# First layer's down projection by seven block products, its weight sums by DMA, conditioning sums re-spread

## The chip, the core and the metric

The kernel runs on one core of one Trainium2 chip. It works with five engines: TensorE (PE in the profile, its weight loads PEld), VectorE (DVE), ScalarE (ACT), GpSimd (POOL) and SyncE (SP), which here only issues transfers. The metric is the time of one execution on the device in microseconds (us). It is read two ways: as the median of unprofiled runs, and from one profiled execution, whose span runs from the first to the last instruction.

## What is computed

Two layers of a diffusion backbone on 512 tokens of width 1024, all float32. Layer 0 mixes the tokens by a long convolution and by neighbourhood attention, layer 1 by a conformer convolution; behind each follows a ConvFFN. Cut to what matters here:

```python
def conv_ffn(t, w_up, w_dw, b_dw, w_down):
    z = dwconv(t @ w_up, w_dw, b_dw)
    g, u = jnp.split(z, 2, axis=-1)
    return (jax.nn.silu(g) * u) @ w_down

for layer in range(DEPTH):
    shift1, scale1, gate1, shift2, scale2, gate2 = adaln_params(c, w_mod[layer], b_mod[layer])
    hn = rms_norm(h, g_mix_pre[layer]) * (1 + scale1) + shift1
    ...
    h = h + gate1 * rms_norm(y, g_mix_post[layer])
    hn = rms_norm(h, g_ffn_pre[layer]) * (1 + scale2) + shift2
    y = conv_ffn(hn, ffn_w_up[layer], ffn_w_dw[layer], ffn_b_dw[layer], ffn_w_down[layer])
    h = h + gate2 * rms_norm(y, g_ffn_post[layer])
```

The inner width D_FF is 2816 = 22 x 128, so the down projection multiplies 512 x 2816 by 2816 x 1024.

## The kernel before

**Products in three matmuls.** A float32 operand is split into a high and a low part of a faster format, and a product is taken as high x high + high x low + low x high (`mm3`, L285 to L289). So each block product of 128 x 128 by 128 x 512 is three matmuls on TensorE, on lines L287, L288 and L289.

**Weights.** They come as a stream `ws` of units of 128 x 1024 floats (512 KB): `load` (L298) has SP bring a unit from memory into one of three `raw` tiles, and `split` (L306, L310) has ACT write the high part and DVE the low part, into a pool `w` of eight tiles. `ws.get(n)` hands out the next unit and splits n more ahead. Loads of the conditioning use the same three `raw` tiles.

**Conditioning.** Shifts, scales and gates are products of one vector with a matrix. They are not done on TensorE but as sums on DVE (`gemv_acc`, L489), one 512 KB load and one instruction for each piece, so that they lie beside other work. `mod_cols` makes shift and scale (loads named wcol), `mod_gate` a gate (loads named wgate, a bias row `binit`, a gain `gp`). They are generators in a list `bg`; `bg_step()` advances the first one by a step, and calls of it are strewn over the program.

**Stages.** After the prologue: the mixer's up projection (to about 135 us, with the norm of 256 context tokens in between), the filter transforms, the attention (about 222 to 291), its output projection (to 345), the first layer's ffn (up projection to 583.4, down projection to 704.9), the conformer (to 857), the second layer's ffn (up projection 865 to 1122, down projection to 1228). In the attention each of 16 units of work has scores on TensorE, an exponential on ACT, a normalisation of the tile P on POOL (L1293) in two halves, transposes of P on TensorE (L1299) and the product with V; TensorE's order is written out by hand there.

**The down projection, two ways.** In the first layer it is `gemm_td`: 22 weight units, for each 4 chunks of tokens x 2 halves of the width x 3 matmuls, with the last six units kept so that the chunks finish one after the other. In the second layer it is `down_fast`, a scheme of seven products instead of eight (Strassen's, in Winograd's form): tokens, inner width and output width are halved, and seven products of half-size blocks, combined by additions, replace eight. Each product runs through 11 pieces of the inner width x 2 token chunks x 3 matmuls, `parts` splits the activations for them (tiles named gs), and DVE and ACT add the results (m, s6, sx, sw) to y. It needs sums of activation blocks, which `blocks` makes on DVE during the up projection (tiles ee and dd, and gu in place), and four sums of weight blocks.

**Weight sums.** `sums_down` makes these in memory by transfers alone: SP copies a block (L358) into a buffer, and POOL issues a transfer that adds a second block onto it (L363), 24 copies and 24 accumulating transfers in six column groups. It is a generator in `bg`, too, and runs during the second layer's up projection. POOL's transfer waits until its copy has landed. POOL and SP take their instructions in order, so what stands behind a waiting instruction waits as well.

**Who orders.** Apart from stretches ordered by hand (the attention and `down_fast` on TensorE), a scheduler places instructions on each engine mainly in the order of the program.

## Time and profile before

| | us |
|---|---|
| median of 3 runs | 1240.96 (1240.25 to 1241.71) |
| the profiled execution | 1239.77 |
| its span | 1238.0 |
| first layer: up projection | about 345 to 583.4 |
| first layer: down projection | 583.4 to 704.9 |
| second layer: up projection | about 865 to 1122 |
| second layer: down projection | 1122 to 1228 |

The granted TensorE clock is 0.997 over the span. 203.55 MB move by DMA, 164 GB/s in the mean, most of it weights. Rows of the timeline have start, length, engine, line, operation, output <- input with shapes, a count where neighbours were put together, and in brackets the idle time before and what ended it. An engine's name with a q (SPq) is its instruction queue, where transfers are issued. A transfer's row on SP or POOL is the time to issue it; it lands later.

### The profile page before, as it was taken

How to read it: one execution, taken by the hardware profiler on the slowest of the kernel's cores; microseconds unless marked ns; L12 is line 12 of the kernel's file. 1: busy time of each engine (PE TensorE's matmuls, PEld its weight loads, DVE VectorE, ACT ScalarE, POOL GpSimd, SP SyncE). 2: the span in 40 equal slices, each digit the busy share in tenths (PEclk: the TensorE clock that was granted, in tenths of full speed). 3: DMA queues.
4: the chain of work that ended last, by engine and by line, in shares of the span. 5: the costliest groups of instructions: out<-in, count | busy, mean ns of one | idle time of the engine just before them, and what ended most of it. 6: DMA issues, size and time to landing. Idle time of an engine off the chain costs nothing.

```text
span 1238.0 us, 15798 instructions
## 1 busy us (share of the span) xinstructions
PE 1222.3 (99%) x6024; PEld 1016.8 (82%) x6024; DVE 872.7 (70%) x1203; ACT 539.0 (44%) x856; POOL 104.7 (8%) x175
## 2 busy tenths in 40 slices
PE   9999999999999999999999999999999999999996
PEld 6688888888898888888888888888988888888885
DVE  6577795876657788878624656787688665667677
ACT  6543334575443333345324443233453333346554
POOL 3300000231200000000000100001100111110002
PEclk9999999999999999999999999999999999999998
DMA  9546334843126477765335152022258889864663
GB/s 349 206 131 190 122 102 139 255 160 120 52 86 221 157 252 253 240 203 170 102 110 180 50 182 68 4 66 86 69 202 240 244 249 250 234 180 136 188 204 128
DMA packets 57883, 203.55 MB, mean 164 GB/s; under 512 B 6859, under 2 KB 6987, under 8 KB 57808
## 3 DMA queue, kind: packets, MB, share of 16 engines
q1 hardware_dynamic: 53988, 190.29, 46.4%
q0 software_dynamic: 3632, 11.93, 5.5%
q8 instruction: 47, 0.77, 0.3%
q10 hardware_dynamic: 188, 0.33, 0.1%
q14 instruction: 28, 0.23, 0.1%
HBM read 199.64 MB, written 25.17 MB: 182 GB/s over the span
## 4 chain that ended last, share of the span: by engine, by line
PE 86%; DVE 7%; DMA 4%; issue 2%; ACT 1%; POOL 0%; SPq 0%; DVEq 0%; POOLq 0%; ACTq 0%
PE pz L287 15%; PE pz L288 15%; PE pz L289 15%; PE acc L289 5%; PE acc L287 5%; PE acc L288 5%; PE pg L287 2%; PE pg L288 2%; PE pg L289 2%; DMA raw<-in_wcol 2%; PE m L287 2%; PE m L288 2%; PE m L289 2%; PE po L1319 1%; DVE w L310 1%
## 5 line engine op out<-in xcount | busy, mean ns | idle before, releaser
L288 PE MATMUL pz<-hTl,w 128*128 128x512 f32 (+1 forms) x920 | 345.4, 376 | 0.0
L287 PE MATMUL pz<-hTh,w 128*128 128x512 f32 (+1 forms) x920 | 344.7, 377 | 0.5 <-DVE hTh L580 0.5
L289 PE MATMUL pz<-hTh,w 128*128 128x512 f32 (+1 forms) x920 | 345.1, 376 | 0.0
L310 DVE TENSOR_TENSOR w<-raw,w 128x1024 fp32r<-128x1024 f32 x179 | 215.0, 1205 | 172.9 <-ACT w L306 170.7
L306 ACT CAST w<-raw 128x1024 fp32r<-128x1024 f32 x179 | 185.0, 1037 | 322.8 <-PE pz L288 139.6
L289 PEld LDWEIGHTS pz<-hTh,w 128*128 128x128 f32 x920 | 173.8, 189 | 31.4
L288 PEld LDWEIGHTS pz<-hTl,w 128*128 128x128 f32 x920 | 173.8, 189 | 30.1 <-DVE hTl L581 0.4
L287 PEld LDWEIGHTS pz<-hTh,w 128*128 128x128 f32 x920 | 173.0, 189 | 31.0 <-DVE hTh L580 1.0
L489 DVE SCALAR_TENSOR_TENSOR acc<-raw,sc,acc 128x1024 f32<-128x1024 f32 x74 | 95.0, 1284 | 39.6 <-DMA raw<-in_wcol 24.5
L1024 ACT ACTIVATE cv<-pz,pk 128x512 f32<-128x512 f32 x88 | 67.6, 772 | 7.7 <-PE pz L289 7.7
L1026 DVE SCALAR_TENSOR_TENSOR cv<-pz,pk,cv 128x511 f32<-128x511 f32 x88 | 65.6, 747 | 1.7
L1025 DVE SCALAR_TENSOR_TENSOR cv<-pz,pk,cv 128x511 f32<-128x511 f32 x88 | 65.2, 745 | 0.3 <-ACT cv L1024 0.2
L1424 ACT ACTIVATE cv<-cv 128x512 f32<-128x512 f32 x44 | 27.7, 629 | 80.1 <-DVE cv L1026 80.0
L287 PE MATMUL m<-w,gs 128*128 128x512 f32 x132 | 51.3, 389 | 0.0
L288 PE MATMUL m<-w,gs 128*128 128x512 f32 x132 | 51.3, 389 | 0.0
L289 PE MATMUL m<-w,gs 128*128 128x512 f32 x132 | 51.3, 389 | 0.0
L310 DVE TENSOR_TENSOR wk<-raw,wk 128x1024 fp32r<-128x1024 f32 (+1 forms) x30 | 35.9, 1205 | 21.8 <-ACT wk L306 21.5
L288 PE MATMUL acc<-w,gs 128*128 128x512 f32 x128 | 49.8, 389 | 0.0
L289 PE MATMUL acc<-w,gs 128*128 128x512 f32 x128 | 49.1, 389 | 0.0
L287 PE MATMUL acc<-w,gs 128*128 128x512 f32 x128 | 48.5, 389 | 0.0
L306 ACT CAST wk<-raw 128x1024 fp32r<-128x1024 f32 (+1 forms) x30 | 30.9, 1037 | 37.4 <-DMA raw<-in_wdn 13.7
L458 POOL TENSOR_SCALAR t<-t,t 128x1 f32<-128x1 f32 x19 | 10.3, 541 | 398.0 <-ACT py L467 389.4
(364 smaller groups left out, 2103.2 us busy)
## 6 DMA issues: line engine op xcount, KB each, us to landing
raw<-in_wup SPq DMA_DIRECT2D x88, 512.0 KB, 4.2
raw<-in_wcol SPq DMA_DIRECT2D x48, 512.0 KB, 4.2
raw<-in_wgate SPq DMA_DIRECT2D x32, 512.0 KB, 4.2
raw<-in_pw SPq DMA_DIRECT2D x24, 512.0 KB, 4.1
raw<-in_wdn SPq DMA_DIRECT2D x22, 512.0 KB, 3.6
raw<-in_win SPq DMA_DIRECT2D x20, 512.0 KB, 3.6
b<-in_wdb SPq DMA_DIRECT2D x20, 512.0 KB, 8.0
raw<-b SPq DMA_DIRECT2D x20, 512.0 KB, 3.6
```

Source lines behind the costliest of these rows:

```text
L287: PE.matmul(o, ah, bh, start=start, stop=False)
L288: PE.matmul(o, ah, bl, start=False, stop=False)
L289: PE.matmul(o, al, bh, start=False, stop=stop)
L306: A.copy(hi, r)
L310: V.tensor_tensor(lo, r, f(hi), op=ALU.subtract)
L458: G.tensor_scalar(v, sums[0], sums[1], EPS, op0=ALU.add, op1=ALU.add)
L489: V.scalar_tensor_tensor(acc, rs[k], ck_, init if k == 0 else acc, op0=ALU.mult, op1=ALU.add)
L1024: A.activation(dst, pz, AF.Identity, bias=pc(bk, i), scale=pc(wk + "1", i))
L1025: V.scalar_tensor_tensor(dst[:, 1:w], pz[:, 0:w - 1], pc(wk + "0", i), dst[:, 1:w], op0=ALU.mult, op1=ALU.add)
L1026: V.scalar_tensor_tensor(dst[:, 0:w - 1], pz[:, 1:w], pc(wk + "2", i), dst[:, 0:w - 1], op0=ALU.mult, op1=ALU.add)
L1319: PE.matmul(po[HALF[e], qs], vt[:, d0:d0 + 64], PT[u // 2][:, e, c, qs], start=first, stop=last)
L1424: A.activation(cv[:, 0], cv[:, 0], AF.Silu, bias=0.0, scale=1.0)
```

## The change

The first layer's down projection also goes by `down_fast`. For this its weights are laid out in blocks as the second layer's are, `sums_down` takes the layer as an argument, and a generator `sums0` of the first layer's sums is advanced by its own calls, from the mixer's up projection to the first layer's up projection. The products of the first layer run in another order ("6213475" against "6217345"; the digits name the seven products). `blocks` now runs in both layers. The two gates and the shift and scale that are computed during the first layer's ffn change places (both gates first), fewer steps are taken per weight unit from the sixteenth step on, a gate's sum accumulates in the tile of its bias, and the gain gp is loaded later. The end of the first layer's ffn allocates the next stage's transposed tiles later (`room`).

```diff
-    wdn = g["ffn_w_down"].reshape(2, NFF, P, D)
-    a["wdn"] = wdn[:1]
-    a["wdb"] = wdn[1].reshape(11, 2, P, 2, 512).transpose(1, 3, 2, 0, 4).reshape(2, 2, P, 11 * 512)
+    wdn = g["ffn_w_down"].reshape(2, 11, 2, P, 2, 512)
+    a["wdb"] = wdn.transpose(0, 2, 4, 3, 1, 5).reshape(2, 2, 2, P, 11 * 512)
...
-    def sums_down():
+    def sums_down(l):
-        b = a["wdb"]
+        b, to = a["wdb"][l], wsum[l]
...
-    PRODUCTS = ("b11_21", "b11_12_21_22", "b11_21_22", (0, 0), (1, 1), "b21_22", (0, 1))
+    PRODUCTS = {"6": "b11_21", "2": "b11_12_21_22", "1": "b11_21_22", "7": (0, 0), "3": (1, 1), "4": "b21_22", "5": (0, 1)}
+    ORDER = ("6213475", "6217345")
...
-        acc = s4(F32, (P, 1024), "acc")
+        acc = s4(F32, (P, 1024), "acc") if init is None else init
...
-        gp = s4(F32, (P, 1024), "gp")
-        SP.dma_start(gp, a["gpost"][l, which - 1].partition_broadcast(P))
         acc = None
         for acc in gemv_acc(a["wgate"][l, which - 1], 8, sc, init=binit):
             yield
+        gp = s4(F32, (P, 1024), "gp")
+        SP.dma_start(gp, a["gpost"][l, which - 1].partition_broadcast(P))
...
+    sums0 = sums_down(0)
+
+    def sums0_step():
+        next(sums0, None)
...
             got.append(u_ev(n, pz))
             bg_step(1)
+            sums0_step()
...
         bg_step(2 if u in (5, 9) else 1)
+        sums0_step()
...
+    bg += [mod_gate(0, 2), mod_gate(1, 1), mod_cols(1, (1, 2))]
...
-            if fast and i % 2:
+            if i % 2:
                 blocks(i // 2)
...
-                bg_step(nbg)
-            if fast and i == NFF - 3:
+                bg_step(nbg - (gi and i >= one))
+                sums0_step()
+            if i == NFF - 3:
                 act_fast(0, 0, keep=True)
+        for _ in sums0:
+            pass
...
-        def act(k):
-            t_ = s4(F32R, n="gs")
-            src = gu[k // 2][:, k % 2]
-            A.copy(t_[:, 0], src)
-            V.tensor_tensor(t_[:, 1], src, f(t_[:, 0]), op=ALU.subtract)
-            return t_[:, 0], t_[:, 1]
-
         bg_drain()
-        gemm_td(NFF, KEEP, act, after, nxt)
+        with tc.manual_schedule(engines={mybir.EngineType.PE}):
+            down_fast(after)
-    bg += [mod_gate(0, 2), mod_cols(1, (1, 2)), mod_gate(1, 1)]
-    after, late2, st2 = stage_end(0, 2, 1, 1)
-    ffn(0, hT, late, after, 4, 2)
+    after, late2, st2 = stage_end(0, 2, 1, 1, room=2)
+    ffn(0, hT, late, after, 4, 2, one=16)
```

What this moves on the engines is shown at four places. First the beginning of the first layer's down projection on PE (lines L286 to L288 after the change are L287 to L289 before); w tiles are weights, gs tiles activations, acc and m are sums in PSUM. Before:

```order
L287 MATMUL acc_5173<-w_5079,gs_5164 128x512
L288 MATMUL acc_5173<-w_5080,gs_5164 128x512
L287 MATMUL acc_5177<-w_5079,gs_5164 128x512
L288 MATMUL acc_5177<-w_5080,gs_5164 128x512
L287 MATMUL acc_5181<-w_5079,gs_5164 128x512
```

and after:

```order
L286 MATMUL m_5284<-w_5179,gs_5091 128x512
L287 MATMUL m_5284<-w_5180,gs_5091 128x512
L288 MATMUL m_5284<-w_5179,gs_5091 128x512
L286 MATMUL m_5284<-w_5179,gs_5091 128x512
L287 MATMUL m_5284<-w_5180,gs_5091 128x512
```

One weight unit served eight sums (acc) before; it serves two (m) now, in a product that has only half of the tokens and of the width. Over the stage the rows with a gs tile go from 528 to 462 (990 to 924 with the second layer's).

Next POOL in the attention. P are the tiles of exponentials that it normalises, qL rows it clears, b_21_0_78 and b_22_0_79 two of the first layer's weight sums. Before:

```order
L1241 MEMSET qL_2229 64x512 x2
L1293 TENSOR_SCALAR P_2106<-P_2106,t_2159 128x512 x2
L1293 TENSOR_SCALAR P_2154<-P_2154,t_2196 128x512 x2
L1293 TENSOR_SCALAR P_2191<-P_2191,t_2289 128x512 x2
L1293 TENSOR_SCALAR P_2284<-P_2284,t_2323 128x512 x2
L1293 TENSOR_SCALAR P_2318<-P_2318,t_2377 128x512 x2
L1241 MEMSET qL_2444 64x512 x2
```

and after:

```order
L1248 MEMSET qL_2247 64x512 x2
L1300 TENSOR_SCALAR P_2123<-P_2123,t_2176 128x512 x2
L363 DMA b_21_0_78<-in_wdb 128x1024
L1300 TENSOR_SCALAR P_2171<-P_2171,t_2214 128x512 x2
L363 DMA b_22_0_79<-in_wdb 128x1024
L1300 TENSOR_SCALAR P_2209<-P_2209,t_2307 128x512 x2
L1300 TENSOR_SCALAR P_2302<-P_2302,t_2342 128x512 x2
L1300 TENSOR_SCALAR P_2337<-P_2337,t_2396 128x512 x2
L363 DMA b_21_0_78<-in_wdb 128x1024
L1248 MEMSET qL_2465 64x512 x2
```

Accumulating transfers now stand between the normalisations of the fourth, fifth and sixth unit and behind that of the eighth.

The copies for which these wait are on SP; raw tiles are loads of wout and wcol, BM the attention's bias. Before:

```order
L298 DMA raw_2141<-in_wcol 128x1024
L1257 DMA BM_2360<-in_rpb 128x1024
L298 DMA raw_2178<-in_wcol 128x1024
L298 DMA raw_2271<-in_wout 128x1024
L298 DMA raw_2486<-in_wout 128x1024
L298 DMA raw_2853<-in_wout 128x1024
```

and after:

```order
L297 DMA raw_2158<-in_wcol 128x1024
L297 DMA raw_2195<-in_wcol 128x1024
L1264 DMA BM_2379<-in_rpb 128x1024
L297 DMA raw_2289<-in_wout 128x1024
L358 DMA b_21_0_78<-in_wdb 128x1024
L358 DMA b_22_0_79<-in_wdb 128x1024
L297 DMA raw_2507<-in_wout 128x1024
L358 DMA b_21_22_0_80<-in_wdb 128x1024
L358 DMA b_12_21_22_0_81<-in_wdb 128x1024
```

The copies come behind the first wout load (raw_2271 before, raw_2289 after) and behind the next one.

Last POOL in the mixer's up projection, at the two context norms (t tiles of one column: a sum and its power of -1/2). Before:

```order
L515 MEMSET binit_768 128x1024
L460 TENSOR_SCALAR t_779<-t_777 128x1
L462 TENSOR_TENSOR t_781<-t_779,nhalf 128x1
L460 TENSOR_SCALAR t_787<-t_785 128x1
L462 TENSOR_TENSOR t_789<-t_787,nhalf 128x1
```

and after:

```order
L514 MEMSET binit_772 128x1024
L363 DMA b_21_0_78<-in_wdb 128x1024
L459 TENSOR_SCALAR t_782<-t_780 128x1
L363 DMA b_22_0_79<-in_wdb 128x1024
L461 TENSOR_TENSOR t_784<-t_782,nhalf 128x1
L459 TENSOR_SCALAR t_790<-t_788 128x1
L461 TENSOR_TENSOR t_792<-t_790,nhalf 128x1
```

One accumulating transfer now stands ahead of the first norm and one in the middle of it.

More of the change, by code (lines that the diff above doesn't have):

```diff
@@ L488, in gemv_acc @@
             else:
-                V.scalar_tensor_tensor(acc, rs[k], ck_, init if k == 0 else acc, op0=ALU.mult, op1=ALU.add)
+                V.scalar_tensor_tensor(acc, rs[k], ck_, acc, op0=ALU.mult, op1=ALU.add)
             yield acc
@@ L648, in gemm_td, with stage_end @@
             after(t, acc[t])
-    def stage_end(l, which, nl=None, nwhich=None, last=False, pre=None):
+    def stage_end(l, which, nl=None, nwhich=None, last=False, pre=None, room=0):
         st_ = {}
         def after(t, acc):
-            if t == 0 and not last:
+            if t == room and not last:
                 st_["hT"] = alloc_hT()
@@ L1414, in backbone_kernel, with ffn @@
         return
-    def ffn(l, hT, late, after, nxt, nbg, fast=False):
+    def ffn(l, hT, late, after, nxt, nbg, one=NFF, last=False):
         mark(f"ffn{l}")
@@ L1480, in prod @@
                 for g in range(6):
-                    w_ = ws.get((2, 2, 2, 2, 2, 4, 4)[q])
+                    w_ = ws.get((2, 2, 2, 2, 2, 4, 4)[q] if last else 2)
                     held.append((g, act_fast(q, g), w_))
@@ L1484, in prod @@
                         between[g]()
-                    if q == 6 and 2 <= g < 5:
+                    if q == 6 and g == 5:
+                        ws.ahead(nxt)
+                    if q == 6 and (2 if last else 3) <= g < 5:
                         continue
```

95 lines of the change are left out of this document (46 added, 49 removed).

## The prediction

> **What bounds the kernel now.** I read the page first: the busy times, then the chain of work that ended last.
>
> ```profile
> PE 1222.3 (99%) x6024; PEld 1016.8 (82%) x6024; DVE 872.7 (70%) x1203; ACT 539.0 (44%) x856; POOL 104.7 (8%) x175
> PE 86%; DVE 7%; DMA 4%; issue 2%; ACT 1%; POOL 0%; SPq 0%; DVEq 0%; POOLq 0%; ACTq 0%
> ```
>
> TensorE is busy 1222.3 of 1238.0 us and carries 86% of the chain. So a matmul that goes is worth its time wherever TensorE stays fed, and a wait of TensorE costs its full length. Whether it stays fed is read stage by stage, from windows: stretch, its length, busy time of PE, PEld, DVE, ACT and POOL with counts, granted clock, DMA share, GB/s.
>
> ```profile
> core 0: us, PE busy (x) PEld busy (x) DVE busy (x) ACT busy (x) POOL busy (x), PEclk, DMA share, GB/s
> 230.00:291.00 61.00, 59.88 (x515) 51.41 (x513) 48.28 (x117) 43.02 (x99) 23.40 (x36) 1.00 0.51 160
> 424.70:513.80 89.10, 89.10 (x395) 73.78 (x394) 74.64 (x79) 28.48 (x35) 0.96 (x1) 1.00 0.75 246
> 583.40:704.90 121.50, 121.50 (x546) 100.76 (x545) 59.44 (x72) 46.93 (x71) 4.16 (x10) 1.00 0.34 105
> 948.52:1024.68 76.16, 76.16 (x338) 63.03 (x337) 49.39 (x67) 27.68 (x35) 9.07 (x11) 1.00 0.88 241
> 1035.56:1046.44 10.88, 10.88 (x50) 9.01 (x49) 7.67 (x11) 4.09 (x6) 0.81 (x1) 1.00 1.03 295
> 1121.00:1228.00 107.00, 106.30 (x468) 87.38 (x466) 81.84 (x120) 62.97 (x109) 5.15 (x6) 1.00 0.55 173
> ```
>
> The first layer's down projection (583.4 to 704.9) is TensorE without a gap. The second layer's, already in seven products (from 1121 on), is 106.30 of 107.00. So the scheme that the change copies runs here at TensorE's pace, and the place that it goes to is bound by TensorE.
>
> **The gain.** The old down projection has 22 x 4 x 2 x 3 = 528 matmuls, seven products have 7 x 22 x 3 = 462: 66 fewer. The instruction order agrees, with 990 PE rows that read a gs tile before and 924 after. For the price of one, the tile views of both forms (duration min/median/max, first and last start):
>
> ```profile
> L287 PE MATMUL m<-w,gs x132: 389/389/389, 1122.1 to 1211.2; 128*128 128x512 f32 x132
> L287 PE MATMUL acc<-w,gs x128: 389/389/389, 583.4 to 669.8; 128*128 128x512 f32 x128
> ```
>
> A record is 0.389 us long, but they overlap. One of the three lines starts 132 times in 89.1 us, so 131 x 3 steps of 89.1/393 = 0.2267 us; the old form gives 86.4/381 = 0.2268. The gain is 66 x 0.2267 = **15.0 us**, if nothing new makes TensorE wait. Everything else is what the new work costs elsewhere.
>
> **Sums in the attention.** The 24 copies (SP) and 24 accumulating transfers (POOL) that build the weight sums are the second layer's procedure, called a second time. POOL runs its instructions in order, and one accumulating transfer now stands between the fourth and the fifth normalisation of P. It waits for its copy to land; the copy stands on SP behind a wout load.
>
> ```profile
> 245.11 5.25 SPq L298 DMA_DIRECT2D raw<-in_wout  x3
> 245.25 1.36 POOL L1293 TENSOR_SCALAR P<-P,t 128x512 f32<-128x512 f32 x2 [1.24 <-DVE t L1291]
> 250.82 1.03 PE L1299 MATMUL pt<-ident,P 128*128 128x128 f32 x8
> 944.35 1.20 SPq L358 DMA_DIRECT2D b<-in_wdb  x2
> 949.79 0.98 POOL L363 DMA_DIRECT2D b<-in_wdb  x1 [61.78 <-DMA b<-in_wdb]
> 956.37 1.14 SPq L358 DMA_DIRECT2D b<-in_wdb  x2
> 963.85 0.81 POOL L363 DMA_DIRECT2D b<-b  x1 [12.01 <-DMA b<-in_wdb]
> ```
>
> In the second layer POOL got past its wait 949.79 - 944.35 = 5.4 us and 963.85 - 956.37 = 7.5 us after the copies' issue. Here the copy is issued at 245.11 + 0.34 = 245.45. It lands at 250.9 to 252.9, POOL spends 0.81 on its own transfer and 0.68 on the first half of the normalisation, and TensorE's transposes, at 250.82 before, start at 252.4 to 254.4: a wait of 1.6 to 3.6, say 2.6. The later transfers of that stage meet normalisations with more room; I add 0.4. **Cost 3.0** (0 if the copy lands before 249.3, 5 if the later waits add up).
>
> The Trainium skill speaks against the placing too: DMA: Bandwidth & Descriptors, section "Issuing engines are not separate DMA queues", says that transfers started by SP, ACT and POOL interleave on the same 16 DMA engines, so a POOL transfer is no free one. By it the sums would slow the weight loads. The trace shows the sharing (share 0.88 and 1.03 in the windows with sums) and no wait of TensorE from it: 76.16 of 76.16 and 10.88 of 10.88. By the rule some us would be added wherever the share passes 1; by the rows nothing.
>
> **Sums in the up-projection.** Two accumulating transfers now stand at the two context norms on POOL, one ahead of the first and one in the middle of it.
>
> ```profile
> 69.93 0.33 SPq L298 DMA_DIRECT2D raw<-in_wgate  x1
> 76.03 0.23 POOL L460 TENSOR_SCALAR t<-t 128x1 f32<-128x1 f32 x1 [15.97 <-ACT junk L467]
> 78.50 0.75 DVE L557 TENSOR_SCALAR junk<-cx,t 128x1024 f32<-128x1024 f32 x1 [0.77 <-POOL t L462]
> 80.02 0.60 PE L1001 MATMUL pt<-ident,junk 128*128 128x128 f32 x4
> ```
>
> Their copies go out behind the wgate load of 69.93, at about 70.3 and 70.9, and land 5.4 to 7.5 later, at 75.7 to 78.4. With two transfers of 0.81, the normalisations end 0.5 to 2.6 later than before; about 0.7 of that is free, since DVE is done at 79.25 and TensorE reads at 80.02. **Cost 0.8** (0 to 2).
>
> **Sums beside the conditioning loads.** Before the attention the chain of waits runs over loads of wcol (start, length).
>
> ```profile
> 150.50 3.40 DMA raw<-in_wcol
> 196.86 5.96 DMA raw<-in_wcol
> 238.62 0.39 PE L1272 MATMUL sc<-kX,qX 128*128 128x256 f32 x1 [1.01 <-ACT PT L1307]
> ```
>
> Two pairs of copies now share the DMA engines with them. The same load takes 3.40 and 5.96 us, so a crowded one is up to 2.6 us late, and TensorE's only wait there, at 238.62, is 1.0 us: part of a delay is absorbed. **Cost 1.0** (0 to 4).
>
> **The up-projection of the first layer.** It gains the block sums of the gated values on DVE, one set for each two steps, eleven in all. The second layer's rows (count, busy time, mean ns):
>
> ```profile
> L1443 DVE TENSOR_TENSOR ee<-gu 128x512 f32<-128x512 f32 x10 | 6.9, 690 | 0.3
> L1444 DVE TENSOR_TENSOR dd<-gu 128x256 f32<-128x256 f32 x10 | 4.2, 418 | 0.0
> L1445 DVE TENSOR_TENSOR gu<-gu 128x256 f32<-128x256 f32 x10 | 4.2, 418 | 0.0
> L1446 DVE TENSOR_TENSOR gu<-gu 128x256 f32<-128x256 f32 x10 | 4.2, 419 | 0.0
> 424.61 1.22 DVE L310 TENSOR_TENSOR w<-raw,w 128x1024 fp32r<-128x1024 f32 x1
> 519.41 1.22 DVE L310 TENSOR_TENSOR w<-raw,w 128x1024 fp32r<-128x1024 f32 x1 [0.88 <-ACT w L306]
> ```
>
> That is 11 x (0.69 + 3 x 0.42) = 21.4 us, 0.49 for each of 44 weight units. DVE has it: 74.64 of 89.10 us busy in the stretch with the most conditioning. What cannot be given away is the lead of the weight splits. With two wcol loads for each unit, 15 splits took 519.41 - 424.61 = 94.8 us, 6.32 each, where TensorE needs 24 x 0.2267 = 5.44. Counted back from 583.4, unit 18 started at 441.96 and unit 33 at 523.5; their splits were done at 425.8 and 520.6. The lead fell from 16.1 to 2.9 us. After the change such a stretch holds 13 units, and then about 1.4 loads for each: 13 x 0.88 = 11.4 us of lead go, 17.8 if DVE's 0.49 adds in full. **Cost 0.3** (0 to 4).
>
> **The end of the down projection.** Two of the four chunks' outputs now come early and two at the end, with DVE as full as at 1212 to 1228 in the second layer; what follows (the conformer's first matmuls on chunks 0 and 1) is refilled by the scheduler. In the second layer the same products lost 0.7 us (107.00 less 106.30). **Cost 0.7** (0 to 3). The gate accumulated in place and the later load of gp remove buffers and no time on the chain; the wait that this could add, for a free tile of the pool, lies on SP and under TensorE's lead.
>
> **Sum.** -15.0 + 3.0 + 0.8 + 1.0 + 0.3 + 0.7 = -9.2. The profiled execution took 1239.77 us (span 1238.0), so it would be 1230.6. The median shown is 1.2 us above that execution: 1240.96 - 9.2 = **1231.8**.
>
> The granted clock is 1.00 in every window above, so none of these waits is priced with a slower clock. The Trainium skill (TensorE: Matmul & The Clock Gate, section "What's actually happening") says that the clock halves after an idle window of about 3.4 us and needs as long to come back; an estimate from that page is 1.7 us more for a wait in the attention that passes 3.4 us. No gap of that length lies inside this trace.
>
> **The rivals.**
> 1. All new waits are covered and the full gain arrives: 1240.96 - 15.0 = 1226.0. For it speaks that the second layer does the same with no loss; against it that its POOL has nothing else to do meanwhile, where the attention's has. Chance 0.20, for under 1228.5.
> 2. The forecast, 1228.5 to 1236. Chance 0.55.
> 3. The splits of the up-projection run out of lead: with 17.8 us used of 16.1, and the copies of the last sums taking DMA time in the same stretch, TensorE waits for each further unit by up to 6.81 - 5.44 = 1.4 us; over three to seven units that is 4 to 10 us beyond the forecast, 1236 to 1242. Chance 0.18.
> 4. Slower than before: POOL's queue in the attention. If copies land there as loads did where many were queued, each wait is much longer. The medians from issue to landing:
>
> ```profile
> b<-in_wdb SPq DMA_DIRECT2D x20, 512.0 KB, 8.0
> land<-in_wmod SPq DMA_DIRECT2D x16, 512.0 KB, 10.6
> ```
>
> At 12 us the first wait is 245.45 + 12 + 0.81 + 0.68 - 250.82 = 8.1, and the two later groups of copies, each about 5 behind its normalisation, give 5 and 5: 18 us, more than the 15.0 gained, so 1240.96 + 3 to 1246. It decides from a summed wait of 15 us on; the stage's DMA share of 0.51 speaks against it. Chance 0.07.
> That the change does not do what it says is excluded by the count of matmuls.
>
> **Range and chances.** 1226.0 (all costs nothing) to 1239.0 (the forecast with every cost near its upper end, and most of rival 3). What a measurement of this kernel can tell from no change is about 0.2%, 2.5 us: faster is under 1238.5, slower over 1243.4. Faster: 0.20 + 0.55 + most of rival 3 = 0.86. Within: the top of rival 3 and the lower part of rival 4, 0.08. Slower: 0.06.
>
> **What would show it.** Right: the products of the first layer start 0.227 us apart and last 105 us; TensorE's wait at the fifth set of transposes is 1.6 to 3.6 us, put down to POOL. The forecast fails if TensorE shows no wait in the attention (then it is rival 1), if splits in the up-projection are followed by waits of TensorE for w (rival 3), or if POOL's accumulating transfers in the attention start 10 us and more behind their copies (rival 4).

## The result and the profile after

The changed kernel is slower: a median of 1257.87 us in 4 runs (1256.57, 1256.94, 1258.79, 1266.62) against 1240.63 of the kernel before in 4, ratio 1.0152 with a 95% interval of 1.0106 to 1.0199. The profiled execution took 1256.57, with a span of 1254.8. The forecast was 1231.8, its range 1226.0 to 1239.0.

The busy times and the chain by engine, from the page of the changed kernel:

```profile
PE 1220.5 (97%) x5958; PEld 1009.1 (80%) x5958; DVE 926.4 (74%) x1321; ACT 567.1 (45%) x918; POOL 131.2 (10%) x199
PE 62%; DVE 15%; DMA 14%; issue 4%; ACT 2%; POOL 1%; SPq 0%; DVEq 0%; POOLq 0%; ACTq 0%
```

The 66 matmuls are gone (6024 to 5958), yet TensorE's busy time fell by 1.8 us and not by 15.0, since matmuls that are left took longer, 6.3 us of it in the attention, where the clock fell (below). Its share of the chain fell from 86 to 62%; DVE and DMA took its place. Windows of the changed kernel show where (stretch, its length, busy PE, PEld, DVE, ACT and POOL with counts, granted clock, DMA share, GB/s): the attention's beginning in two pieces, the rest of it, the first layer's up projection and its down projection.

```profile
222.00:240.00 18.00, 14.61 (x100) 13.40 (x99) 8.83 (x20) 6.66 (x15) 2.75 (x4) 0.93 0.79 210
240.00:260.00 20.00, 16.56 (x108) 13.59 (x107) 18.17 (x36) 13.73 (x30) 8.11 (x14) 0.93 0.84 295
260.00:300.00 40.00, 37.00 (x304) 31.98 (x304) 22.95 (x67) 23.60 (x58) 18.21 (x28) 0.90 0.78 219
350.70:606.60 255.90, 249.62 (x1194) 207.58 (x1193) 206.90 (x259) 95.84 (x129) 11.84 (x16) 1.00 0.71 220
606.60:719.80 113.20, 110.03 (x480) 89.12 (x480) 89.88 (x139) 69.46 (x122) 7.68 (x10) 0.98 0.57 179
```

The same up projection in the kernel before:

```profile
336.30:583.40 247.10, 246.84 (x1194) 208.51 (x1193) 192.24 (x221) 96.72 (x129) 3.60 (x6) 1.00 0.60 196
```

So three places lost: the attention (clock 0.90 to 0.93, DMA share about 0.8), the up projection (255.9 us for the same 1194 matmuls as in 247.1) and the down projection (113.2 us, where 462 x 0.2267 and 1.9 of transposes would be 106.6).

The table cuts every profiled span at the same places: the first P transposes of the attention, the first matmul with wout, the first matmul of the first layer's down projection, the start of the conformer, the end. It gives each stage's length minus that of the kernel before, in us; the product with wout counts with the up projection that follows it. Runs other than "after" are the experiments below. Each row is one execution, and executions of one kernel differ: e2's eight runs lie between 1243.09 and 1252.95 and its profiled one is the slowest, and the kernel before has medians from 1240.63 to 1242.83 beside the different experiments. So a difference of 1 or 2 us in one cell is not read as an effect.

| run | up to the attention | attention | up projection | down projection | rest | span, sum |
|---|---|---|---|---|---|---|
| after | +2.4 | +12.0 | +8.8 | -8.3 | +1.9 | +16.8 |
| e1_no_sums | +1.7 | 0.0 | +6.3 | -11.7 | +0.4 | -3.3 |
| e2_hold_accum | +5.1 | +2.7 | +17.0 | -13.3 | +1.7 | +13.2 |
| e3_no_blocks | +5.6 | +8.6 | +10.4 | -6.5 | +0.6 | +18.7 |
| e4_gate_in_conf | +6.9 | +11.3 | +11.8 | -11.5 | +18.1 | +36.6 |
| e5_even | +3.1 | +9.2 | +25.6 | -11.1 | +1.4 | +28.2 |
| e6_early_sums | +19.4 | +0.5 | +4.7 | -8.0 | +2.5 | +19.1 |
| e7_early_even | +19.4 | +1.4 | +18.8 | -12.9 | +3.3 | +30.0 |
| e8_raw4 | +12.1 | +7.4 | -0.1 | -14.8 | +1.3 | +5.9 |
| e9_no_sums_blocks | +2.3 | -1.3 | +5.3 | -7.4 | +2.0 | +0.9 |
| e10_old_cond | +1.2 | +9.5 | +11.1 | -12.6 | +2.2 | +11.4 |
| e11_raw4_hold | +6.4 | -1.3 | +0.2 | -14.8 | +3.3 | -6.2 |
| e12_raw4_fit | +1.8 | -1.3 | +0.2 | -14.3 | +2.7 | -10.9 |
| e13_before_raw4 | -1.3 | -1.6 | 0.0 | 0.0 | +1.3 | -1.6 |

**The attention.** First the chain of waits ahead of it, of the kernel before and of the changed one (start, length), then the changed kernel's timeline of P transposes and weight sums (start, length, engine, line, operation, and in brackets the idle time before it and what ended it):

```profile
217.74 4.72 DMA raw<-in_wcol
223.80 3.50 DMA raw<-in_wcol
```

```profile
216.74 9.94 DMA raw<-in_wcol
226.70 1.29 DVE acc L488
228.01 5.90 DMA raw<-in_wcol
234.01 1.28 DVE acc L488
235.37 0.59 DVE P L1292
```

```profile
212.00 1.14 SPq L358 DMA_DIRECT2D b<-in_wdb  x2
236.29 0.66 PE L1306 MATMUL pt<-ident,P 128*128 128x128 f32 x4 [2.93 <-POOL P L1300]
251.26 1.17 SPq L358 DMA_DIRECT2D b<-in_wdb  x2
256.44 0.84 POOL L363 DMA_DIRECT2D b<-in_wdb  x1 [3.99 <-DMA b<-in_wdb]
258.07 1.33 PE L1306 MATMUL pt<-ident,P 128*128 128x128 f32 x5 [1.12 <-POOL P L1300]
272.07 1.12 POOL L363 DMA_DIRECT2D b<-b  x1
285.72 0.83 POOL L363 DMA_DIRECT2D b<-b  x1 [8.52 <-DVE t L1292]
286.30 3.60 POOL L1300 TENSOR_SCALAR P<-P,t 128x512 f32<-128x512 f32 x5
287.34 1.97 PE L1306 MATMUL pt<-ident,P 128*128 128x128 f32 x8 [3.00 <-POOL P L1300]
```

Two mechanisms, three waits. At 217, behind two copies issued at 212.00, a wcol load took 9.94 us, where the loads at this place took 4.72 and 3.50 before (and 4.94 and 3.59 in e1 below, which has no sums); DVE's accumulation of the conditioning waits for it, and DVE's P step stands behind that accumulation. At 256.44 and 285.72 it is POOL. At 256.44 its transfer had waited 3.99 us for the copy. The one at 285.72 adds a block that the transfer of 272.07 writes, so it can go only when that one has landed. The tile view of the two transfers issued at 271.52 and 272.07 gives their landing:

```profile
DMA to landing us min/median/max: 9.2/11.3/13.4
```

The 9.2 is that of 271.52, so that of 272.07 landed 13.4 us after its issue, at about 285.5, and POOL went on 0.2 us later. Five normalisations of P were queued behind it and then ran without a gap (286.30). The timeline names DVE as that wait's releaser, which ended at 285.51, at the same moment within what can be read; e2 below, where these transfers are gone from the attention and the wait with them, settles it.

TensorE's waits sum to less than was lost. By the list of waits (engine, line and tile, what was waited for, us in all, times, longest) they are:

```profile
PE pt L1306 <- POOL P L1300: 7.1, 3, 3.0
PE sc L1279 <- DVE t L1292: 2.1, 2, 1.2
```

The first of 2.93 us lies ahead of the first transposes, so 6.3 us of these waits stand behind them, where the stage lost 12.0. From the first transposes to the first matmul with wout, before and after:

```profile
233.95:291.00 57.05, 55.93 (x482) 47.46 (x480) 44.95 (x113) 42.11 (x95) 22.50 (x34) 1.00 0.48 150
236.29:305.40 69.11, 62.20 (x480) 52.07 (x480) 48.20 (x117) 42.67 (x97) 28.04 (x41) 0.90 0.75 225
```

TensorE's idle time there rose from 1.1 to 6.9 us, and its busy time by 6.3 for the same matmuls (482 and 480 records), at a clock of 0.90 in place of 1.00. So half of the stage's loss is waits and half is clock. Windows of the changed kernel ahead of the first wait, behind it, behind the second and behind the third:

```profile
228.00:232.00 4.00, 4.00 (x35) 4.00 (x35) 0.59 (x2) 0.82 (x2) 0.00 (x0) 1.00 0.84 137
236.00:240.00 4.00, 3.24 (x15) 2.70 (x16) 3.96 (x10) 2.12 (x5) 1.49 (x3) 0.70 0.93 218
257.00:261.00 4.00, 2.93 (x18) 2.60 (x20) 3.91 (x11) 2.92 (x8) 3.86 (x6) 0.64 1.02 388
288.00:292.00 4.00, 4.00 (x29) 3.29 (x29) 0.69 (x1) 2.00 (x5) 2.56 (x4) 0.50 0.62 123
```

At 288 TensorE is busy throughout at a granted clock of 0.50. Against the kernel before, the transposes are late by 2.3 us at the first set, by 4.5 two sets on, by 7.3 at the fifth, by 8.9 after that, by 12.0 at the eleventh and by 14.4 at the last: behind the three waits 2.2, 1.6 and 2.4 us more were lost (smaller waits of 0.46 and 0.86 us have a part in the first).

**The up projection.** The timeline of TensorE there and in the down projection holds many small waits for weight splits, of which these are three:

```profile
543.43 0.50 PE L286 MATMUL pz<-hTh,w 128*128 128x512 f32 x1 [0.51 <-ACT w L305]
557.75 0.50 PE L288 MATMUL pz<-hTh,w 128*128 128x512 f32 x1 [1.32 <-DVE w L309]
618.86 0.50 PE L287 MATMUL m<-w,gs 128*128 128x512 f32 x1 [0.83 <-DVE w L309]
```

The lead of the splits over TensorE (from the end of a unit's split on DVE to the unit's first matmul) is gone from about 540 on and isn't won back before the down projection, which starts without it. Counting the 44 units from 0, unit 27 was split by 496.80 and started at 504.68, a lead of 7.9 us; unit 33 was split by 537.52 and started at 537.32, so it had none.

### The profile page after: what moved, and what is told of

Read it like the earlier page. It is cut to its first block, busy times and chain, and to the rows that moved or that the text cites. A ratio compares the mean times of both kernels' runs of the same rounds, so it can differ in the third digit from the quotient of the medians.

```text
span 1254.8 us, 16002 instructions
## 1 busy us (share of the span) xinstructions
PE 1220.5 (97%) x5958; PEld 1009.1 (80%) x5958; DVE 926.4 (74%) x1321; ACT 567.1 (45%) x918; POOL 131.2 (10%) x199
## 3 DMA queue, kind: packets, MB, share of 16 engines
q0 software_dynamic: 7088, 23.47, 10.5%
## 4 chain that ended last, share of the span: by engine, by line
PE 62%; DVE 15%; DMA 14%; issue 4%; ACT 2%; POOL 1%; SPq 0%; DVEq 0%; POOLq 0%; ACTq 0%
PE pz L286 9%; PE pz L287 9%; PE pz L288 9%; DMA raw<-in_wcol 5%; PE m L287 4%; PE m L288 4%; PE m L286 4%; DVE w L309 4%; DMA raw<-in_wgate 3%; PE pg L286 2%; PE pg L288 2%; PE pg L287 2%; DMA raw<-in_wup 2%; PE acc L288 2%; PE acc L287 2%
## 5 line engine op out<-in xcount | busy, mean ns | idle before, releaser
L305 ACT CAST w<-raw 128x1024 fp32r<-128x1024 f32 (+1 forms) x205 | 208.7, 1024 | 329.5 <-PE pz L287 142.3
L288 PE MATMUL pz<-hTh,w 128*128 128x512 f32 (+1 forms) x920 | 346.1, 377 | 4.7 <-DVE w L309 4.7
L309 DVE TENSOR_TENSOR w<-raw,w 128x1024 fp32r<-128x1024 f32 (+1 forms) x205 | 242.0, 1186 | 141.8 <-ACT w L305 140.2
L286 PE MATMUL pz<-hTh,w 128*128 128x512 f32 (+1 forms) x920 | 344.9, 377 | 1.3 <-DVE hTh L583 0.5
L287 PE MATMUL pz<-hTl,w 128*128 128x512 f32 (+1 forms) x920 | 345.5, 377 | 0.0
L288 PEld LDWEIGHTS pz<-hTh,w 128*128 128x128 f32 x920 | 173.8, 189 | 39.1 <-DVE w L309 8.0
L286 PEld LDWEIGHTS pz<-hTh,w 128*128 128x128 f32 x920 | 173.0, 189 | 32.6 <-ACT w L305 1.7
L287 PEld LDWEIGHTS pz<-hTl,w 128*128 128x128 f32 x920 | 173.9, 189 | 30.2 <-DVE hTl L584 0.4
L287 PE MATMUL m<-w,gs 128*128 128x512 f32 x286 | 112.7, 394 | 1.9 <-DVE w L309 1.7
L286 PE MATMUL m<-w,gs 128*128 128x512 f32 x286 | 112.1, 392 | 1.3 <-ACT w L305 1.3
L288 PE MATMUL m<-w,gs 128*128 128x512 f32 x286 | 112.0, 392 | 0.0
L488 DVE SCALAR_TENSOR_TENSOR acc<-raw,sc,acc 128x1024 f32<-128x1024 f32 x46 | 59.2, 1286 | 29.0 <-DMA raw<-in_wcol 28.9
L287 PEld LDWEIGHTS m<-w,gs 128*128 128x128 f32 x286 | 54.0, 189 | 15.2 <-DVE w L309 4.1
L286 PEld LDWEIGHTS m<-w,gs 128*128 128x128 f32 x286 | 54.1, 189 | 13.1 <-ACT w L305 1.7
L288 PEld LDWEIGHTS m<-w,gs 128*128 128x128 f32 x286 | 54.1, 189 | 11.1
L488 DVE SCALAR_TENSOR_TENSOR binit<-raw,sc,binit 128x1024 f32<-128x1024 f32 x32 | 41.0, 1282 | 27.4 <-DMA raw<-in_wgate 25.7
L457 POOL TENSOR_SCALAR t<-t,t 128x1 f32<-128x1 f32 x19 | 16.4, 864 | 362.1 <-ACT py L466 354.9
L363 POOL DMA_DIRECT2D b<-b x24 | 20.0, 834 | 284.3 <-DMA b<-in_wdb 183.8
```

What stands on the lines that cost most here:

```text
L286: PE.matmul(o, ah, bh, start=start, stop=False)
L287: PE.matmul(o, ah, bl, start=False, stop=False)
L288: PE.matmul(o, al, bh, start=False, stop=stop)
L305: A.copy(hi, r)
L309: V.tensor_tensor(lo, r, f(hi), op=ALU.subtract)
L363: G.dma_start(to[n][:, cs], src[:, cs], accum_op=ALU.add)
```

## The experiments

Two theories stood against each other at first. **A**: the weight sums did it, by POOL's and the DMA engines' queues in the attention. **B**: DVE's block sums and the re-spread conditioning did it, by eating the lead of the splits. A third candidate, the ring of three raw tiles, stands in their expectations from the first. Each ratio is taken to runs of the kernel before beside it. e1, e3, e9 leave work out or read plain blocks in place of sums.

**e1, no sums.** The first layer's products read block 11 in place of the sums, and no sum is formed.

```diff
-            src = wsum[l][n] if isinstance(n, str) else a["wdb"][l, n[0], n[1]]
+            src = a["wdb"][l, 0, 0] if l == 0 else wsum[l][n] if isinstance(n, str) else a["wdb"][l, n[0], n[1]]
...
-    sums0 = sums_down(0)
+    sums0 = iter(())
```

> The changed kernel without the first layer's weight sums: none of their copies and accumulating transfers is issued, and the four products that would read a sum read the plain block b11 instead, as many bytes (so those products are not the reference's). Theory A, that the sums cause the loss before and in the attention (15.1 us there by the milestones of the two traces): the last transposes of P come at or before 288.5 us instead of 302.9, and the time is 1257.9 - 15 = 1243, less 1 to 3 more if the sums also slow the first layer's up-projection. Rival, that the loss there comes from the moved conditioning work or the other edits: the attention stays 10 us or more late, time over 1252. By both, the up-projection of the first layer (8.8 us over before) keeps at least 5 us of its loss if the ring of raw tiles is its cause.

Median 1236.48, ratio 0.9957 (0.9935 to 0.9979). The attention is back at its old length. The tile view of the transposes (duration in ns min/median/max, first and last start), of the kernel before, of the change and of e1:

```profile
L1299 PE MATMUL pt<-ident,P x128: 270/272/329, 233.9 to 288.5; 128*128 128x128 f32 x128
```

```profile
L1306 PE MATMUL pt<-ident,P x128: 270/273/476, 236.3 to 302.9; 128*128 128x128 f32 x128
```

```profile
L1306 PE MATMUL pt<-ident,P x128: 270/273/328, 235.6 to 290.2; 128*128 128x128 f32 x128
```

54.6, 66.6 and 54.6 us. The long matmul of 476 ns, the slow clock's mark, is gone too. So the attention's loss is the sums'. The up projection, however, still loses 6.3 us: A doesn't cover that.

**e2, accumulations held.** The sums' accumulating transfers of the attention stand in a list and are issued only behind the last normalisation of P; the copies go as before.

```diff
-                        G.dma_start(to[n][:, cs], src[:, cs], accum_op=ALU.add)
+                        if hold[0] and l == 0:
+                            held.append((to[n][:, cs], src[:, cs]))
+                        else:
+                            G.dma_start(to[n][:, cs], src[:, cs], accum_op=ALU.add)
...
+            with tc.issue_after(norm[0]):
+                G.dma_start(o, i, accum_op=ALU.add)
...
```

> The changed kernel with the copies where they are, but every accumulating transfer of POOL from the V projection to the end of the attention put behind the last normalisation of P. If POOL's order is the cause inside the attention: the transposes lose only what they had lost at the first unit, +2 to +5 us against before instead of +14.4, and no wait of TensorE in the attention is put down to POOL; time about 1248 to 1250. If the copies' and accumulations' use of the DMA engines is the cause, wherever POOL issues them: +10 us or more stay at the last transposes, time over 1254. The wait ahead of the first unit (loads of wcol beside the copies at 212 us) should stay in both, at 3 us.

Median 1249.98, ratio 1.0049 (1.0025 to 1.0073). The transposes take 57.3 us in place of 66.6:

```profile
L1317 PE MATMUL pt<-ident,P x128: 270/273/329, 239.0 to 296.3; 128*128 128x128 f32 x128
```

So 9.3 of the 12.0 came with the accumulating transfers that stood in POOL's queue between normalisations. (e2 takes their traffic out of the attention, too, but the copies' traffic stays, and the rows at 256.44 and 286.30 above show normalisations waiting in the queue.) One wait of 2.6 us for P is left, at the end of a chain of wcol loads. But the up projection now loses 17.0 us, since the held transfers fall into it: much of what was taken from one stage came back in the next.

**e3, no block sums.** The up projection of the first layer forms no block sums on DVE, and its products read plain blocks.

```diff
-            if i % 2:
+            if l and i % 2:
```

> The changed kernel without the block sums of the activations in the first layer (blocks is left out there, products 3, 4 and 5 read plain blocks, so they are not the reference's): 21 us of DVE work less in the up-projection. If DVE is what slows the weight splits there: the up-projection takes at most 3 us more than before (238.4) instead of 8.8, and the down projection's first two products lose their waits too; time about 1249. If the three raw tiles and the loads are the bound: the up-projection keeps 6 us or more of the loss, time 1255 to 1258.

Median 1257.64, ratio 1.0129 (1.0092 to 1.0165). The up projection loses 10.4 us without them: DVE's 21.4 us of block sums are not its cause, and B's first half falls.

**e4, the second layer's first gate later.** It leaves the up projection for the conformer.

```diff
-    bg += [mod_gate(0, 2), mod_gate(1, 1), mod_cols(1, (1, 2))]
+    bg += [mod_gate(0, 2), mod_cols(1, (1, 2))]
...
+    bg += [mod_gate(1, 1)]
```

> The changed kernel with the conformer's gate (8 loads and 8 sums on DVE) computed during the conformer instead of the first layer's up-projection, so that there are 56 conditioning loads in the up-projection instead of 64 less 8. If the ring of raw tiles is the bound of the up-projection (2.1 us a load): 8 loads less give 17 us of it, the lead is not used up, the up-projection's loss falls from 8.8 to under 2 and the waits at the start of the down projection go; time 1246 to 1250. If the ring is not the bound: loss as it was, time 1256 to 1260. If the conformer has no room for it, its stages grow by what the up-projection gains.

Median 1276.32, ratio 1.0279 (1.0246 to 1.0312). The waits of TensorE have one large one, in the conformer, where the gate was asked for before its work had been spread:

```profile
PE pm L530 <- ACT ga L305: 14.1, 1, 14.1
```

That is the experiment's own flaw. The up projection still loses 11.8 us with eight loads fewer in its conditioning, and by the expectation this speaks against the ring of raw tiles. Its trace shows why it doesn't: the 32 wcol loads, two for each weight unit through most of them, now run from 428 to 547 us, and there the time is lost.

```profile
428.00:547.00 119.00, 112.56 (x476) 90.50 (x476) 97.86 (x119) 35.95 (x45) 6.51 (x8) 0.97 0.83 256
```

TensorE is idle for 6.4 us in this window, and for 0.3 and 0.8 in what the stage has ahead of it and behind it. The eight loads were taken from where there was room.

**e5, an even spread.** The point from which the up projection takes one conditioning step for each unit, and no longer two, moves.

```diff
-    ffn(0, hT, late, after, 4, 2, one=16)
+    ffn(0, hT, late, after, 4, 2, one=11)
```

> The changed kernel with one number other: the conditioning gets three steps for two weight units instead of four from the 11th step of the up-projection on (not the 16th). Sums and blocks as they are. If the loss of the first layer's up-projection (8.8 to 10.4 us) is the raw ring running out of lead because two conditioning loads ride on each weight unit: the lead stays positive, the stage loses 2 to 5 us, and the waits at the start of the down projection shrink; time 4 to 7 us under the changed kernel, about 1251. If the sums' copies in that stage cost the lead on their own: 8 us or more stay.

Median 1266.1, ratio 1.0193 (1.0172 to 1.0214). The last conditioning sum came too late, and half of the stage's loss is one wait for it:

```profile
PE pm L501 <- DVE acc L488: 12.6, 1, 12.6
```

The other 13 us remain: against the expectation (2 to 5 us), spreading the same loads otherwise doesn't create room.

**e6, the sums early; e7, early and even.** All sums go between the context norms and the second Fourier step, four steps at a time; e7 is e6 with e5's edit.

```diff
+    def sums0_step(n=1):
+        for _ in range(n):
+            next(sums0, None)
...
-            sums0_step()
+            if i:
+                sums0_step(4)
...
```

> The changed kernel with all copies and accumulating transfers of the first layer's sums between the context norms (about 80 us) and the second Fourier step (about 170 us), where POOL has nothing else to do; none beside the last loads of wcol, in the attention or in the up-projection. If place is what made them dear: the attention loses 0 to 3 us, the first layer's up-projection loses what it loses without sums (6.3), the whole is as fast as the run without sums, 1236 to 1239. If the sums cost by their traffic wherever they are: the mixer's projections up to 230 us lose 8 us or more by slower weight loads, time over 1245.

> Both edits together: sums between the context norms and the second Fourier step, three conditioning steps for two weight units from the 11th step on. If the two causes are separate and these are their places, the gains add: attention 0 to 3 us late, up-projection 0 to 3, down projection 12 to 14 us shorter than before; time 1229 to 1234, faster than before. If there is a third cause in the down projection itself (loads, splits), its gain stays near 8 to 12 and the time is 1235 to 1240.

Medians 1259.53, ratio 1.014 (1.012 to 1.016), and 1268.11, ratio 1.0205 (1.0188 to 1.0222). The attention is free, and the mixer ahead of it loses 19.9 us, as the rival in e6's expectation had it; in e7 the two remedies don't add. The mixer's window in e6, and behind it that of the same stretch in the kernel before:

```profile
56.30:252.10 195.80, 184.55 (x875) 152.98 (x874) 133.14 (x170) 71.13 (x109) 29.72 (x38) 0.97 0.83 246
```

```profile
56.80:232.70 175.90, 175.65 (x875) 149.34 (x874) 133.12 (x171) 70.33 (x109) 8.81 (x13) 1.00 0.46 143
```

A DMA share of 0.46 became 0.83, and TensorE's idle time 0.25 us became 11.25. Room by share was there; the weight loads that this stretch lives on were late all the same: in the median win landed after 7.3 us and wv after 10.6, against 3.6 and 3.5 before.

After these seven, every form of the up projection had lost its lead, with the sums or without, with the blocks or without. **Theory C**: the lead was used up in the kernel before already, and what limits the splits is the ring of three raw tiles through which every weight load and every conditioning load passes. In the crowded stretch the prediction counted 15 splits in 94.8 us; with their two wcol loads that is 45 loads, 2.1 us each, 6.3 us for each tile of three. In the kernel before, from 424.6 to 519.4, a wup load landed after 3.6 us (median) and was read by ACT for 1.05 and then by DVE for 1.22; a wcol load landed after 4.6 and was read by DVE for 1.28. Both make 5.9, with the 0.33 that SP takes to issue at most 6.2: of 6.3, next to nothing to spare. The waits of SP's own queue in this stretch (what it waited for, us in all, times, longest) say the same, in the kernel before:

```profile
SPq L298 <- DVE acc L489: 38.4, 30, 1.4
SPq L298 <- DVE w L310: 26.8, 15, 2.6
```

DVE's reading of a conditioning load or of a weight unit is what frees a raw tile. 30 + 15 waits stand against 45 loads: load for load, SP waited for a tile of the ring.

**e8, four raw tiles.** One tile of the pool "s" pays for it.

```diff
-    rpool = ctx.enter_context(tc.tile_pool(name="raw", bufs=3))
-    spool = ctx.enter_context(tc.tile_pool(name="s", bufs=31))
+    rpool = ctx.enter_context(tc.tile_pool(name="raw", bufs=4))
+    spool = ctx.enter_context(tc.tile_pool(name="s", bufs=30))
```

> The changed kernel with a fourth raw tile (and 30 instead of 31 tiles in the pool of activations, which pays for it). If the first layer's up-projection loses because its 44 weight loads and 64 conditioning loads pass through three raw tiles one behind the other: the stage loses 0 to 3 us instead of 8.8 to 10.4, and the lead of the splits at the last unit is several us; time 1246 to 1250. If the DMA engines or DVE are its bound, a fourth tile changes nothing: loss 8 us or more. The loss before and in the attention may change by a few us, since the loads of wcol there go through the same tiles.

Median 1245.75, ratio 1.0012 (0.9991 to 1.0033). Its windows for the up and the down projection:

```profile
355.80:602.80 247.00, 246.68 (x1194) 208.55 (x1192) 209.74 (x265) 97.76 (x134) 11.81 (x16) 1.00 0.73 230
602.80:709.50 106.70, 106.70 (x481) 88.63 (x481) 86.74 (x134) 68.36 (x117) 8.71 (x10) 1.00 0.59 185
```

With the same sums and block sums, and a higher DMA share than in the change (0.73 against 0.71), the up projection is back at 247.0 and the down projection is TensorE without a gap, 14.8 us shorter than before. C holds. The lines of ACT's casts show the relief from the other side, of the changed kernel and of e8 (busy us, mean ns, idle before, and what ended it):

```profile
L305 ACT CAST w<-raw 128x1024 fp32r<-128x1024 f32 x43 | 45.0, 1049 | 111.6 <-DMA raw<-in_wup 78.7 <-PE pz L287 29.0 <-DMA raw<-b 3.9
```

```profile
L305 ACT CAST w<-raw 128x1024 fp32r<-128x1024 f32 x43 | 45.0, 1049 | 88.9 <-PE pz L287 45.0 <-DMA raw<-in_wup 38.9 <-PE pz L288 5.0
```

Waits for loads halve, from 78.7 to 38.9 us, and most of the rest are for TensorE to free a tile: the splits are ahead. The stages up to the attention (+12.1) and the attention (+7.4) still lose.

**e9, no sums and no block sums** (e1 and e3 together), with three raw tiles.

> The changed kernel without the first layer's weight sums and without its block sums of activations (products read plain blocks, so they are not the reference's): of the change only the seven products and the new order of the conditioning are left. The run without sums kept 6.3 us of loss in the up-projection, the run without block sums 10.4. If the two share the loss (either is enough to use up the lead): under 2 us are left, time 1229 to 1232. If the new order of the conditioning costs it by itself: 5 us or more are left, time 1235 or over.

Median 1241.24, ratio 0.9987 (0.9968 to 1.0006). The up projection:

```profile
337.30:589.70 252.40, 248.52 (x1195) 207.99 (x1193) 191.18 (x217) 94.26 (x128) 3.67 (x6) 1.00 0.58 190
```

5.3 us longer than before, with no more DMA and no more DVE work: what is left of the change there is the new order of the conditioning, with the gate in place. That alone uses up the lead (none is left from unit 38 on, as the wcol loads now run to 575 us).

**e10, the old order of the conditioning**, with sums, blocks and three tiles.

```diff
-    bg += [mod_gate(0, 2), mod_gate(1, 1), mod_cols(1, (1, 2))]
+    bg += [mod_gate(0, 2), mod_cols(1, (1, 2)), mod_gate(1, 1)]
...
-    ffn(0, hT, late, after, 4, 2, one=16)
+    ffn(0, hT, late, after, 4, 2)
```

> The changed kernel with the conditioning in the old order and density (gate, shift and scale, then the conformer's gate; two steps for each unit throughout). Sums and blocks as they are. If the new order is what costs the up-projection its lead at the end: the loss falls under 4 us, time about 1252. If sums and blocks cost it: loss 8 to 14 us, time 1257 to 1263.

Median 1253.79, ratio 1.0102 (1.0076 to 1.0127). The up projection loses 11.1 us, now earlier, where the old order was tightest:

```profile
500.00:520.00 20.00, 17.44 (x65) 13.97 (x64) 16.52 (x19) 6.98 (x9) 0.00 (x0) 0.83 0.82 240
```

So neither order saves it: the sums' copies and block sums push the old order over its limit, and the new order goes over it by itself.

**e11, four raw tiles and held accumulations** (e8 and e2 together).

> Fourth raw tile, and POOL's accumulating transfers behind the last normalisation of the attention. The two remedies act at different places: if both theories hold, the attention loses 2 to 5 us, the up-projection 0 to 4, and the down projection is 12 to 14 us shorter than before; time 1232 to 1238, at least as fast as before. If the held accumulations load the DMA engines in the up-projection (there they had cost 17 us with three raw tiles): time 1242 to 1250.

Median 1234.56, ratio 0.9944 (0.9919 to 0.997), faster than the kernel before. No wait of TensorE for POOL is left in the attention (-1.3), the up projection is at +0.2, and the held transfers that cost 17.0 in e2 cost nothing beside a fourth tile. What remains is the beginning (the mixer's first matmul 4.9 us late) and the conformer (+4.0).

**e12, e11 with a landing place and one table moved.** The start's sixteen conditioning loads take one tile of "s" less, one raw tile more, and two small tables of the conformer share one tile.

```diff
-            where = "ssssssssrrrwwsss"[i]
+            where = "ssssssssrrrrwwss"[i]
...
-    wd = s4(F32, (P, 1024), "wd")
+    wd = kk[:, 512:1024]
...
-    SP.dma_start(wd[:, 0:512], a["wdw"])
+    SP.dma_start(wd, a["wdw"])
```

> The run with four raw tiles and held accumulations, with its two new losses taken back: the prologue (4.9 us late, since a tile of the activation pool is missing there) gets one landing place more in the raw tiles and one less in the activations, and the conformer (4.0 us) puts its two small tables into one tile. If these losses come from the missing tile: the first matmul of the up-projection starts at 57 to 58 us again, the conformer loses 0 to 1, time 1225 to 1230. If the fourth raw tile itself delays the early loads: 1232 to 1236 as it was.

Median 1233.04 (1228.98 to 1234.53), ratio 0.9934 (0.9913 to 0.9955): the best form found, which computes the whole reference. The mixer's first matmul is back at -0.7; the conformer's +4.1 did not move, so the table was not its cause, and the time missed the 1225 to 1230 expected. Its windows for the attention's beginning and later part, and for the up and the down projection:

```profile
222.00:240.00 18.00, 17.56 (x127) 16.41 (x126) 14.39 (x30) 10.69 (x22) 2.72 (x4) 1.00 0.73 235
260.00:300.00 40.00, 40.00 (x338) 33.65 (x337) 27.14 (x63) 26.36 (x55) 16.12 (x23) 1.00 0.49 131
336.80:584.10 247.30, 246.71 (x1195) 208.43 (x1193) 211.33 (x268) 99.23 (x138) 14.19 (x18) 1.00 0.71 229
584.10:691.30 107.20, 107.13 (x480) 88.33 (x481) 90.07 (x139) 70.20 (x124) 8.65 (x10) 1.00 0.58 187
```

The granted clock is 1.00 in all four.

**e13, the kernel before with four raw tiles** and the same two places.

> The kernel before with the same four raw tiles and the same two places: eight products, no sums for the first layer. It has no wait of TensorE that the ring causes, so a fourth tile should give it nothing: 1238 to 1243. If it gains as much as the changed kernel does, the fourth tile is a gain by itself and the change is worth nothing; if not, the difference to the run beside it is what the seven products are worth once the loads fit (forecast: 12 to 15 us).

Median 1238.83, ratio 0.998 (0.9971 to 0.999). The fourth tile by itself is worth some 2 us, and its up projection is unchanged (0.0), as it had just enough lead. Measured on the same chip, e12 lies 1238.83 - 1233.04 = 5.8 us below it by medians, and 9.3 by the two profiled spans (1236.4 and 1227.1; e12's profiled execution was the fastest of its four). So, given the ring and the late accumulations, the change is worth 6 to 9 of its 15 us, less than the 12 to 15 expected. By the table's rows the rest is lost ahead of the attention (3.1 us between e13 and e12) and behind the down projection (1.4). The conformer's +4.1 stands in e13 as well (from 702.0 to 838.4, where it was 704.9 to 837.2), so it isn't the change's.

## Why the prediction was wrong, step by step

- **The gain, -15.0: right.** With TensorE fed, the down projection is 14.3 to 14.8 us shorter (e8, e11, e12).
- **The way up to the attention, 0.8 and 1.0 in the prediction, 2.4 measured: near, partly by luck.** The context norms, priced at 0.8, cost nothing (TensorE's only wait from 55 to 233 us is one of 0.2 for a weight split). The conditioning loads beside the sums, priced at 1.0, cost the 2.4, within the 0 to 4 given. There the mechanism was the one described, a crowded load; but it was 9.94 us long, where the largest row taken was 5.96.
- **The sums in the attention, 3.0 in the prediction: 12.0 measured.** The place is that of rival 4, at 0.07, but not its mechanism: it let the copies land late (12 us), and the first copy kept POOL for 5.2. The step that failed is "the later transfers of that stage meet normalisations with more room; I add 0.4". The first transfer behaved as forecast: copy at 251.26, POOL past its wait at 256.44, the fifth set of transposes fell back by 2.8 us, with waits of 1.25 and 1.12 (2.6 in the prediction). The later one, an accumulation that must follow another accumulation, was late by the landing of the first, 13.4 us, where the kernel before's accumulations landed after 4.7 to 10.5 (median 6.4, in the second layer). The 0.4 had to cover this chain. And "none of these waits is priced with a slower clock" failed: of the 12.0 us some 6 are clock (busy time 55.9 to 62.2 for the same matmuls), after waits that were all 3.0 us or shorter.
- **DMA sharing at no price: wrong.** "By the rule some us would be added wherever the share passes 1; by the rows nothing" chose the rows, but those rows were of stretches whose loads had lead to lose. e6 shows the opposite where they have none: 19.9 us at a mean share of 0.83, with weight loads landing after 7.3 to 10.6 us. (The limit at a share of 1 is the prediction's own; no run shows such a limit.) In the attention the share rose from 0.48 to 0.75 over the stage and was 1.04 while the late accumulation was under way; what the sharing cost there isn't told apart from POOL's order.
- **The up projection, 0.3 in the prediction: 8.8 measured.** This is rival 3, at 0.18, in its mechanism and about in its size for this stage. The step that failed is "Counted back from 583.4, unit 18 started at 441.96 and unit 33 at 523.5 ... The lead fell from 16.1 to 2.9 us". The count put 0.2267 us for each matmul and left out the matmuls of the conditioning sums, which TensorE runs in between (2.8 us from unit 33 to the end). The trace of the kernel before has the first matmul of unit 33 and such a group behind it:

```profile
520.77 0.39 PE L287 MATMUL pz<-hTh,w 128*128 128x512 f32 x1
526.22 1.84 PE L502 MATMUL pm<-sel,acc 128*128 128x4 f32 x16
```

  The unit started at 520.77, and its split was done at 520.6: a lead of 0.1, not 2.9 (0.6 to its third matmul, the first that reads what DVE makes). The kernel before was at the limit at this unit, and had 3.7 us or more again from the next one on, without a wait to show for it, since 246.84 of 247.10 us busy looks the same with a lead of 0.1 as with one of 10. So every addition cost time: the order of the conditioning (e9), and the sums with the blocks (e10). The rate was too low as well: "13 x 0.88 = 11.4 us of lead go" started from 16.1, where the changed kernel lost 8.1 in the six units from 27 to 33, 1.35 each, and had 7.9 to lose. And no step asked what sets the rate, which is the ring (e8). The prediction's price for the blocks, 0.49 us of DVE for each unit, was not the term that counted (e3).
- **The end of the down projection, 0.7 in the prediction: 6.7 measured** (-8.3 where -15.0 was the gain). It is the same lost lead: with a fourth raw tile the stage is at -14.8. The rest of +1.9 in the later stages is no larger than what single executions differ by.

Sum of what was measured: -15.0 + 2.4 + 12.0 + 8.8 + 6.7 + 1.9 = +16.8, the difference of the spans.

Left open: why the second accumulation took 13.4 us to land (the DMA share was 1.04 from 256.4 to 286.0, but no run separates sharing from the order of POOL's own transfers); why the V projection ends some 2 to 4 us later in kernels that differ only later (its last matmul starts at 205.5 us before, 205.4 in the change, 208.8 in e3, 209.1 in e4, and also at 207.8 in e1, which has no sums); what costs the conformer 4 us in e11 to e13. The wait for the P step behind the conditioning's accumulation on DVE was seen in the chain and was not taken away by itself.

## What to carry to other kernels

Before adding work to a stage where the bounding engine is never idle, measure the lead of what feeds it, for each unit, from the start of that unit's first matmul in the trace rather than by counting: 100% busy says nothing of the reserve. Where loads pass through a ring of few tiles, compare the ring's depth with the landing time and the reading time; one more tile made room for everything that the change added to the up projection. Transfers that wait for one another don't belong in the queue of an engine whose other instructions are due, and a stage freed of them is only a gain if the stage that takes them in has room (e2 against e11).

## What the runs showed of the hardware

- **The clock fell after short waits.** In the attention waits of TensorE of 2.93, 1.12 (behind one of 1.25) and 3.00 us were followed by 4 us windows with a granted clock of 0.70, 0.64 and 0.50, and by 1.6 to 2.4 us of further delay each. The Trainium skill (TensorE: Matmul & The Clock Gate, section "What's actually happening") puts the drop at an idle window of about 3.4 us. None of these waits was that long, so the measurement decides here.
- **A mean DMA share below 1 is no promise.** With 48 transfers of weight sums moved into 196 us, the share rose from 0.46 to 0.83 and the stage lost 19.9 us (e6); a load of wcol that took 3.5 to 4.7 us took 9.94 behind two copies (the change). The share doesn't tell the two apart: it was 0.88 from 216.7 to 226.7 there, and 0.89 beside the load of 4.72 in the kernel before.
- **Accumulating transfers vary.** In the changed kernel they landed after 4.3 to 13.4 us, 6.5 in the median; the one of 13.4 kept POOL's next transfer, and the five normalisations behind it, until 285.72.
